# TensorE's instruction order written by the kernel, and the SSD scan as two lanes with GpSimd scaling x and E

## The chip, the cores and the metric

One core of one Trainium2 chip runs the whole program. The metric is the device time of one execution in microseconds (us). The core has TensorE for matrix products (PE in the profile; PEld is its weight load), VectorE (DVE), ScalarE (ACT), GpSimd (POOL), and SyncE (SP), whose queue issues nearly all transfers. PSUM is the accumulator memory that TensorE writes and the other engines read.

## What is computed

The reference is one layer of a diffusion transformer over 1024 latent tokens that follow 256 context tokens, with 2048 channels. Cut to what matters:

```
u = rms_norm(h, pre_w) * (1 + scale) + shift                  # scale, shift, gate from c @ w_ada
z, xbc, dt, qkv, b, a = split(u @ w_in)                       # latent and context rows
xbc, qkv = silu(centred_dwconv(xbc)), silu(centred_dwconv(qkv))
ssd_y = ssd_scan both directions: 16 heads of 64, 2 groups, state 128, chunks of 128
gdn_o = gdn_scan both directions: 8 heads of 128, chunks of 128, per chunk
        (I + strict lower part)^-1 and then, chunk after chunk,
        v_new = u - w @ S;  o = q @ S + attn @ v_new;  S = S * decay + k^T @ v_new
y = concat(ssd_out_norm(ssd_y, z), gdn_out_norm(gdn_o, z))
out = h_lat + gate * rms_norm(y @ w_out, post_w)
```

Both scans run forward and backward over 10 chunks (2 of context, 8 latent), and the context chunks only give the first state.

## The kernel before

The projection `u @ w_in` is worked out in column blocks of 128: 16 z blocks, 24 GDN blocks (q, k, v of 8 heads) and 12 SSD blocks. A column block has two groups of 512 tokens, and for k, v and most SSD blocks a third of 256. Each group is 48 matmuls into one PSUM bank: 16 row blocks of `w_in`, each as three fp16 products (high and low halves). In the rows they read `ps_d<-u,w` or `ps_e<-u,w` (`group`, `products`, L434 to L445). They are called dense products here. What follows a group is VectorE's and ScalarE's work: the convolution (`conv_block`, L498, L502, L503), the split of the next weight tile (`split`, L408, L411, L413), with six buffers of raw weights, five buffers `cv` of convolved blocks (`CB`), and a few PSUM banks.

The rest of the program is put between those blocks. For each GDN head: `gdn_post` (transposes, norms), `gdn_prep` (decay matrices, L676 to L700), `invert` (a recurrence of many small VectorE steps, L726 and L728, then products L764 to L787), `gdn_chain`, `gdn_end`. `gdn_chain` is the recurrence over chunks, for both directions, `ps_c0` and `ps_c1`. A step of one direction is a round trip between engines, three times over: TensorE multiplies with the state S (L850, L852), VectorE forms `r` (L856); TensorE multiplies the inverse with `r` (L866), VectorE forms `xw` (L871) and ScalarE `r`'s successor (L873); TensorE forms the state's increment from `xw` (L876) and the output from `r` (L888), VectorE the new S (L881).

The SSD scan runs in four quarters of four heads (`ssd_quarter`, L915). A quarter first goes backward over its 10 chunks and then forward. Per chunk: `xtok` transposes x; `state` scales it (`xd`, 4 ScalarE instructions, L941), multiplies (L943), multiplies the old state by its decay on GpSimd (L949) and adds on VectorE (L950); `before` multiplies the state with C (L962) and weighs it (L964). The forward direction also builds the 128x128 decay matrices of 4 heads and both directions, `E` (L984 to L996): a broadcast load per direction, 8 ScalarE instructions that add a bias G (L989), two predicated copies and a product on VectorE (L990, L992, L996), an exponential on ScalarE (L991). Four products use E (L1003), GpSimd and VectorE add their parts to the output (L999, L1006).

```
L938 def state(d, c, H, first):
         xd = t_([P, R, PD], "xd", bufs=3)
         for r in range(R): nc.scalar.activation(out=xd[:, r], in_=xs[:, c, r], func=AF.Copy, scale=...)
L982     E = t_([P, 2, R, P], "E", bufs=2)
         for d in range(2): for r in range(R):
L989         nc.scalar.activation(out=E[:, d, r], in_=E[:, d, r], func=AF.Identity, bias=...)
```

`build` (L1201) writes the program as a list of steps (block, post, prep, invert, chain, end, quarter, norm), one wholly behind the other. A scheduler then decides, from costs that it models, in which order each engine gets its instructions, TensorE included; each engine works its own list strictly in that order and waits where an operand is missing. At the end `y @ w_out` is done in 8 column groups of 256 (L1138), with the weights `u<-in_w_out_dram` read and split as before.

## Time and profile before

| what | value |
|---|---|
| median of 3 runs | 2355.13 us (2354.93 to 2360.46) |
| the profiled execution | 2351.73 us, span 2350.0 us |
| mean granted TensorE clock | 0.978 |
| TensorE busy | 2162.5 us, 92% of the span |
| VectorE busy | 1399.5 us, 60% |
| ScalarE busy | 998.5 us, 42% |
| GpSimd busy | 268.7 us, 11% |

The GDN heads lie between about 411 and 1477 us, the SSD scan between about 1500 and 2056 us, and the last product behind that. A wait is put down to the instruction that released it. A matmul in fp32 has two records, and the ends of matmuls are modelled; their starts are what counts.

### The profile page before, as it was taken

Reading aid. Unit: us, or ns where it says so; the run is one execution under the profiler, and the core shown is the slowest. Engines: PE = TensorE matmul, PEld = TensorE weight load, DVE = VectorE, ACT = ScalarE, POOL = GpSimd, SP = SyncE. Lnnn points to the kernel's source line nnn. Section 1 sums busy time; section 2 is a strip of 40 time slices with the busy share of each in tenths; the row PEclk is TensorE's granted clock in tenths of the full one; section 3 lists DMA queues with packets and bytes.
Section 4 is the critical chain, followed back from the end, with each engine's and each line's share of the span. In section 5 each row is a group of like instructions: output and inputs, shape, how many; then the busy total and the mean of one; then the engine's idle time right before and its main releaser. Section 6 shows DMA issues by size and latency. Waiting matters only on the chain. (4 is left out here: it accounts for less than half of the span.)

```text
span 2350.0 us, 41855 instructions
## 1 busy us (share of the span) xinstructions
PE 2162.5 (92%) x16070; PEld 1379.2 (59%) x16070; DVE 1399.5 (60%) x3499; ACT 998.5 (42%) x2493; POOL 268.7 (11%) x514
## 2 busy tenths in 40 slices
PE   4989999889999898998989999999999999899998
PEld 4334644456665655556555566555555555788887
DVE  5335543869694856858568486566767773511214
ACT  6026422344444352433524444465667584423320
POOL 1000001012111020111201110130303130000000
PEclk9999999999999999999999999999999999999999
DMA  9952347454444344343443444333465355212117
GB/s 323 348 164 55 80 145 217 117 131 106 134 115 120 101 126 116 88 133 93 121 119 85 127 123 115 99 90 108 111 183 149 98 164 195 68 37 73 55 37 269
DMA packets 397236, 301.71 MB, mean 128 GB/s; under 512 B 61339, under 2 KB 358684, under 8 KB 395628
## 3 DMA queue, kind: packets, MB, share of 16 engines
q1 hardware_dynamic: 386668, 293.80, 43.7%
q10 hardware_dynamic: 10368, 5.24, 0.8%
q8 instruction: 126, 2.06, 0.4%
q14 instruction: 74, 0.61, 0.1%
HBM read 241.41 MB, written 57.57 MB: 127 GB/s over the span
## 5 line engine op out<-in xcount | busy, mean ns | idle before, releaser
L437 PE MATMUL ps_d<-u,w 128*128 128x512 f16 (+1 forms) x4560 | 969.6, 357 | 8.3 <-DVE cv L498 4.6
L437 PEld LDWEIGHTS <-w 128*128 128x128 f16 x6048 | 595.3, 100 | 494.3 <-issue 36.4
L1138 PEld LDWEIGHTS <-u 128*128 128x128 f16 x3072 | 298.7, 98 | 50.9 <-DMA u<-in_w_out_dram 13.2
L437 PE MATMUL ps_e<-u,w 128*128 128x512 f16 (+1 forms) x1296 | 314.5, 376 | 0.0
L498 DVE SCALAR_TENSOR_TENSOR cv<-ps_d,taps,cv 128x496 f32<-128x496 f32 (+3 forms) x300 | 194.8, 650 | 80.0 <-ACT cv L492 38.6
L413 DVE SCALAR_TENSOR_TENSOR w<-w,scl 128x512 f16<-128x512 f32 (+1 forms) x204 | 149.9, 777 | 50.8 <-ACT w L411 50.3
L408 ACT ACTIVATE w<-w 128x1024 f16<-128x1024 f32 (+1 forms) x102 | 106.5, 1044 | 167.7 <-DMA w<-in_w_in_dram 101.5
L1138 PE MATMUL ps_d<-wx,u 128*128 128x256 f16 x1536 | 170.2, 273 | 4.6 <-DMA u<-in_w_out_dram 4.6
L1138 PE MATMUL ps_d<-w,u 128*128 128x256 f16 x1296 | 144.8, 273 | 5.7 <-DMA u<-in_w_out_dram 3.8
L1168 DVE SCALAR_TENSOR_TENSOR raw<-ps_d,inv,gp 128x256 f32<-128x256 f32 x59 | 28.4, 483 | 193.2 <-ACT jko L1166 193.2
L411 ACT ACTIVATE w<-w,scl 128x1024 f16<-128x1024 f32 (+1 forms) x102 | 112.3, 1133 | 36.2 <-DVE scl L145 16.5
L1166 ACT ACTIVATE jko<-ps_d,inv 128x256 f32<-128x256 f32 x59 | 27.8, 471 | 182.4 <-PE ps_d L1138 177.4
L989 ACT ACTIVATE E<-E,G 128x128 f32<-128x128 f32 x256 | 80.9, 388 | 35.1 <-DMA E<-gr 29.6
L690 ACT ACTIVATE gb<-gb 128x256 f32<-128x256 f32 x80 | 32.2, 413 | 147.0 <-DVE gb L676 144.0
L502 ACT ACTIVATE t<-cv 128x512 f32<-128x512 f32 (+1 forms) x98 | 55.7, 570 | 90.0 <-DVE cv L498 75.4
L676 DVE SCALAR_TENSOR_TENSOR gb<-gb,G,mneg 128x128 f32<-128x128 f32 x160 | 50.8, 345 | 69.2 <-DMA gb<-gr 67.9
L873 ACT ACTIVATE r<-ps_c,nb 128x128 f32<-128x128 f32 x128 | 45.7, 364 | 107.0 <-DVE xw L871 97.2
L876 PE MATMUL ps_c<-xw,vq 128*128 128x128 f32 x288 | 61.8, 304 | 30.8 <-DVE xw L871 14.2
L726 DVE TENSOR_TENSOR tp<-X 80x30 f32<-80x30 f32 (+14 forms) x240 | 77.6, 323 | 13.9 <-DMA X<-d 13.2
L876 PEld LDWEIGHTS ps_c<-xw,vq 128*128 128x128 f32 x288 | 47.4, 196 | 58.9 <-ACT r L873 33.7
L503 DVE SCALAR_TENSOR_TENSOR cv<-t,cv 128x512 f32<-128x512 f32 (+1 forms) x98 | 60.5, 618 | 31.7 <-ACT t L502 31.3
L728 DVE TENSOR_TENSOR X<-X,tp 80x30 f32<-80x30 f32 (+14 forms) x240 | 78.4, 327 | 0.6
(329 smaller groups left out, 3250.4 us busy)
## 6 DMA issues: line engine op xcount, KB each, us to landing
w<-in_w_in_dram SPq DMA_DIRECT2D x102, 512.0 KB
x<-in_w_ada_dram SPq DMA_DIRECT2D x48, 1024.0 KB
vq<-vq SPq DMA_DIRECT2D x128, 256.0 KB
E<-gr SPq DMA_DIRECT2D x64, 256.0 KB
u<-in_w_out_dram SPq DMA_DIRECT2D x24, 512.0 KB
gb<-gr SPq DMA_DIRECT2D x80, 128.0 KB
x<-in_x_dram SPq DMA_DIRECT2D x8, 1024.0 KB
vq<-gb SPq DMA_DIRECT2D x64, 128.0 KB
```

Of the source, the lines that this page charges most:

```text
L408: nc.scalar.activation(out=w16[h][:, 0], in_=w[h], func=AF.Square, accum_out=ssq[:, h:h + 1])
L411: nc.scalar.activation(out=w16[h][:, 0], in_=w[h], func=AF.Copy, scale=t)
L413: nc.vector.scalar_tensor_tensor(out=w16[h][:, 1, s], in0=w[h][:, s], scalar=t, in1=w16[h][:, 0, s], op0=ALU.mult, op1=ALU.subtract)
L437: self.nc.tensor.matmul(out=ps, lhsT=w16[k // KH][:, a, k % KH], rhs=self.u16[b][k][:, lo:lo + n], start=(k == 0 and i == 0), stop=(k == K ...
L498: nc.vector.scalar_tensor_tensor(out=o3[:, :, lo_o:hi_o], in0=p3[:, :, lo_o + s:hi_o + s], scalar=taps[tap], in1=o3[:, :, lo_o:hi_o], op0= ...
L502: nc.scalar.activation(out=t[:, 0:n], in_=o, func=AF.Tanh)
L503: nc.vector.scalar_tensor_tensor(out=o, in0=t[:, 0:n], scalar=1.0, in1=o, op0=ALU.add, op1=ALU.mult)
L726: nc.vector.tensor_tensor(out=t, in0=X[:, k + 1:, k:k + 1].to_broadcast(sh), in1=X[:, k:k + 1, 0:k].to_broadcast(sh), op=ALU.mult)
L728: nc.vector.tensor_tensor(out=X[:, k + 1:, 0:k], in0=X[:, k + 1:, 0:k], in1=t, op=ALU.add)
L876: nc.tensor.matmul(out=pS, lhsT=vq[:, 1], rhs=xw, start=True, stop=True)
L989: nc.scalar.activation(out=E[:, d, r], in_=E[:, d, r], func=AF.Identity, bias=self.G[:, j, c:c + 1])
L1138: self.nc.tensor.matmul(out=ps, lhsT=self.y16(k, p, s), rhs=w16[k // 4][:, q, k % 4], start=(i == 0 and j == 0), stop=(i == KB - 1 and j = ...
```

## The change

TensorE's order is no longer the scheduler's. `mix` takes one generator that emits the dense products one at a time (`dense`), and six others, the lanes, that emit everything else. It keeps a clock of TensorE's own work in nanoseconds (`mm` adds 2 + columns/2.4, four times the columns in fp32), and a lane that yields a number gets its next turn when that many nanoseconds of TensorE work have been emitted. So between two dependent products of a lane lie 2500 ns of other products (`CHAIN`), 3200 (`BACK`) or 5500 (`FORTH`) for the SSD chunks, 2400 per chunk in `gdn_prep`, 40000 ahead of an inverse, 11000 in the split of a weight tile. A lane that yields a condition waits until it holds. The other engines are still ordered by the scheduler. Two rules stop the dense products: a convolved block isn't begun while 5 `cv` buffers are held (`live`), and SSD block 10 not before the SSD buffers exist.

The SSD quarter becomes two lanes, so that the backward half of quarter Q+1 runs beside the forward half of quarter Q. GpSimd scales x (`xd`, 72 instructions of 128x256 for 288 of ScalarE) and adds the bias to E (64 of 128x512 for 256 of ScalarE). E has three buffers for the first direction and one, `E1`, for the second. The gate rows load their weights one group ahead and are spread between dense products. The z blocks 0 to 3 move in front of the SSD blocks. TensorE, VectorE and SyncE issue as many instructions as before.

```diff
+CHAIN, BACK, FORTH = 2500, 3200, 5500
 CB = 5
...
+    def mm(self, out, lhsT, rhs, **kw):
+        n = rhs.shape[-1] if len(rhs.shape) == 2 else rhs.shape[-1] * rhs.shape[-2]
+        self.clock += 2 + n * (4 if rhs.dtype == F32 else 1) / 2.4
+        self.nc.tensor.matmul(out=out, lhsT=lhsT, rhs=rhs, **kw)
+    def mix(self, dense, lanes):
+        self.lanes = [[lane, 0.0] for lane in lanes]
+        self.dense_until = None
+        alive = True
+        while alive or self.lanes:
+            moved = False
+            for it in list(self.lanes):
+                if it[1]() if callable(it[1]) else it[1] <= self.clock:
+                    moved = True
+                    try:
+                        r = next(it[0])
+                        it[1] = r if callable(r) else self.clock + r
+                    except StopIteration:
+                        self.lanes.remove(it)
+            if alive and (self.dense_until is None or self.dense_until()):
+                moved = True
+                try:
+                    self.dense_until = next(dense)
+                except StopIteration:
+                    alive = False
...
+            if not moved:
+                later = [it[1] for it in self.lanes if not callable(it[1])]
...
+                self.clock = min(later)
...
         for k in range(KB):
-            self.products(ps, w16, k, lo, n)
+            for i, (a, b) in enumerate(((0, 0), (0, 1), (1, 0))):
+                self.mm(out=ps, lhsT=w16[k // KH][:, a, k % KH], rhs=self.u16[b][k][:, lo:lo + n],
+                        start=(k == 0 and i == 0), stop=(k == KB - 1 and i == 2))
+                yield
...
+        if pool is None:
+            yield lambda: self.live < CB
+            self.live += 1
...
+            px = ps[:, 2 * P:3 * P]
+            self.mm(out=px, lhsT=D["T"][:, d, c], rhs=r, start=True, stop=True)
...
+                nc.vector.tensor_scalar(out=xw, in0=px, scalar1=D["pw"][:, d, c:c + 1], scalar2=None, op0=ALU.mult)
...
+            yield CHAIN
+            if not last:
+                pS = ps[:, 3 * P:4 * P]
+                self.mm(out=pS, lhsT=vq[:, 1], rhs=xw, start=True, stop=True)
...
+        def scaled(d, c):
+            xd = t_([P, R, PD], "xd", bufs=2)
+            nc.gpsimd.tensor_tensor(out=xd, in0=xs[:, c], in1=bc(self.dtw[:, hs[d], c], PD), op=ALU.mult)
+            return xd
...
+        def within(c):
+            s = slice(c * P, (c + 1) * P)
+            E, E1 = t_([P, R, P], "E", bufs=3), t_([P, R, P], "E1")
+            for d in range(2):
+                nc.sync.dma_start(out=(E, E1)[d], in_=self.gr[hs[d], s].partition_broadcast(P))
+            for d in range(2):
+                nc.gpsimd.tensor_tensor(out=(E, E1)[d], in0=(E, E1)[d], in1=bc(self.G[:, hs[d], c], P), op=ALU.add)
+            nc.vector.copy_predicated(out=E, mask=self.mask[:, 1].bitcast(I32).unsqueeze(1).to_broadcast([P, R, P]), data=E1)
...
+        steps += z(0, 1, 2, 3) + s_(8, 0, 1) + [("W", 0)] + s_(10, 2, 3, 9, 4, 5, 11, 6, 7) + z(4, 5, 6)
...
+        def forth_lane():
+            for Q in range(4):
+                yield until(("B", Q))
+                yield from forth[Q]
+                done.add(("F", Q))
+                if Q < 2:
+                    self.live -= 2 + (Q == 1)
...
+        with tc.manual_schedule(engines={mybir.EngineType.PE}):
+            self.mix(dense(), [chain_lane(0), chain_lane(1), heads_lane(), forth_lane(), back_lane(), first_weights()])
```

On TensorE, in a chunk step of the GDN recurrence of a middle head, before. `ps_c` is a recurrence's bank, `ps_e` that of dense products; a row L866 and the row L876 with the same bank number are the round trip over `xw`:

```order
L866 MATMUL ps_c_6166<-r_6169,A 128x128
L437 LDWEIGHTS w
L437 MATMUL ps_e<-u,w 128x512
L437 LDWEIGHTS w
L437 MATMUL ps_e<-u,w 128x512
L437 LDWEIGHTS w
L437 MATMUL ps_e<-u,w 128x512
L437 LDWEIGHTS w
L437 MATMUL ps_e<-u,w 128x512
L437 LDWEIGHTS w
L437 MATMUL ps_e<-u,w 128x512
L876 MATMUL ps_c_6166<-xw_6174,vq_6135 128x128
```

Five dense products stand between the two here; over the 144 such pairs it is 4 to 6 in half of them, and 0 to 3 in 45.

The same engine and the same kind of place now; all of these products are issued by `mm`, L107. It is one such round trip, of bank 10503, in two pieces:

```order
L107 MATMUL ps_c_10503<-r_10506,A 128x128
L107 LDWEIGHTS w
L107 MATMUL ps_e<-u,w 128x512
L107 MATMUL ps_m<-cv 128x128 x2
L107 LDWEIGHTS w
L107 MATMUL ps_e<-u,w 128x512
```

```order
L107 LDWEIGHTS w
L107 MATMUL ps_e<-u,w 128x512
L107 MATMUL ps_c_10496<-xw_10558,vq_10465 128x128
L107 MATMUL ps_c_10496<-r_10557,vq_10465 128x128
L107 LDWEIGHTS w
L107 MATMUL ps_e<-u,w 128x512
L107 MATMUL ps_c_10503<-xw_10565,vq_10473 128x128
```

Between the two pieces lie four more dense products, eight in all. Of the 144 pairs 102 have 8 to 11 dense products in between, and other lanes' products beside them.

On TensorE where the forward half of SSD quarter 0 runs beside the backward half of quarter 1, now. `ps_x<-ident,cv` are transposes, `ps_z` products with the state, `ps_h` state increments from `xd`, `ps_y` products with E:

```order
L101 MATMUL ps_x<-ident,cv 128x128 x2
L107 MATMUL ps_z<-cv,H_16333 128x128 x2
L107 MATMUL ps_h<-xd,btok 128x256
L107 MATMUL ps_z<-cv,H_16377 128x128 x2
L107 MATMUL ps_y<-E,xs 64x128 x4
L107 MATMUL ps_h<-xd,btok 128x256
L107 MATMUL ps_x<-cv 128x128
```

Rows of this kind stand 108 products long with no dense product between them: five `cv` buffers (SSD blocks 8, 0, 1, 2, 3) are held until the forward half is done. Before, no stretch of the scan is without them.

On GpSimd in the forward half of SSD quarter 0, before (`H` is the state's decay, `cv<-y` the addition to the output):

```order
L949 TENSOR_TENSOR H_16035<-H_15992,cd 128x256
L999 TENSOR_TENSOR cv<-y_16012,cv 128x128 x2
L949 TENSOR_TENSOR H_16078<-H_16035,cd 128x256
L999 TENSOR_TENSOR cv<-y_16055,cv 128x128 x2
L999 TENSOR_TENSOR cv<-y_16098,cv 128x128 x2
```

And now, beside the backward half of quarter 1:

```order
L1064 TENSOR_TENSOR E<-E,G 128x512
L1064 TENSOR_TENSOR E_16566<-E_16566,G 128x512
L1035 TENSOR_TENSOR H_16333<-H_16333,cd 128x256
L1025 TENSOR_TENSOR xd<-xs,dtw 128x256 x2
L1112 TENSOR_TENSOR cv<-y_16501,cv 128x128 x2
L1035 TENSOR_TENSOR H_16663<-H_16592,cd 128x256
L1035 TENSOR_TENSOR H_16333<-H_16333,cd 128x256
```

A pair of chunks, one forward and one backward, now has two additions of 128x512, two scalings and two decays of 128x256 and two additions of 128x128 on GpSimd.

## Rows read from the trace of the kernel before

**Rows 1.** The page: busy time of each engine, share, instructions.
```profile
PE 2162.5 (92%) x16070; PEld 1379.2 (59%) x16070; DVE 1399.5 (60%) x3499; ACT 998.5 (42%) x2493; POOL 268.7 (11%) x514
```

**Rows 2.** Busy us of each engine by stretch, granted clock, DMA share, GB/s.
```profile
core 0: us, PE busy (x) PEld busy (x) DVE busy (x) ACT busy (x) POOL busy (x), PEclk, DMA share, GB/s
...
134.00:411.00 277.00, 253.93 (x1896) 135.12 (x1894) 136.53 (x268) 107.57 (x184) 11.87 (x22) 0.94 0.41 120
411.00:1477.00 1066.00, 986.82 (x7622) 614.82 (x7623) 758.78 (x2189) 427.07 (x1120) 150.56 (x296) 0.97 0.44 116
...
1500.00:2056.00 556.00, 524.26 (x3183) 316.45 (x3181) 362.96 (x746) 343.66 (x898) 89.71 (x153) 0.99 0.44 127
```

**Rows 3.** TensorE's waits between 411 and 1500 us: total, times, longest.
```profile
PE ps_c L888 <- DVE S L881: 14.4, 7, 3.3
PE ps_c L876 <- DVE xw L871: 14.2, 5, 3.2
PE ps_m L693 <- DVE gb L700: 13.8, 7, 6.7
PE ps_c L876 <- ACT r L873: 13.4, 8, 3.0
PE ps_s L134 <- ACT w L408: 9.9, 10, 2.0
PE ps_m L787 <- DVE et L777: 5.2, 8, 0.8
PE ps_c L96 <- POOL o L835: 3.4, 2, 2.0
```

**Rows 4.** TensorE between 763 and 770 us: start, us, instruction, count.
```profile
764.10 1.89 PE L437 MATMUL ps_d<-u,w 128*128 128x512 f16 x8
...
768.74 0.41 PE L850 MATMUL ps_c<-S,cv 128*128 128x128 f32 x2
```

**Rows 5.** VectorE in the same stretch.
```profile
768.51 0.35 DVE L856 SCALAR_TENSOR_TENSOR r<-ps_c,eG,vq 128x128 f32<-128x128 f32 x1
768.82 0.61 DVE L697 SCALAR_TENSOR_TENSOR A<-gb,nb,ps_m 128x128 f32<-128x128 f32 x2
769.40 0.35 DVE L856 SCALAR_TENSOR_TENSOR r<-ps_c,eG,vq 128x128 f32<-128x128 f32 x1
```

**Rows 6.** TensorE's waits between 1500 and 2056 us.
```profile
PE ps_z L962 <- DVE H L950: 6.5, 11, 2.3
PE ps_y L1003 <- DVE E L996: 5.6, 7, 2.2
PE ps_d L437 <- DVE cv L498: 4.6, 3, 2.2
PE ps_h L1047 <- DVE dg L1046: 4.4, 4, 1.5
```

**Rows 7.** Busy us in three slices of 58.75 us, columns as in rows 2.
```profile
528.75:587.50 58.75, 57.80 (x352) 36.87 (x352) 54.24 (x168) 26.97 (x66) 13.72 (x26) 1.00 0.40 106
881.25:940.00 58.75, 50.62 (x546) 35.07 (x545) 39.66 (x117) 16.23 (x34) 0.96 (x2) 0.94 0.48 116
1175.00:1233.75 58.75, 47.30 (x456) 33.23 (x455) 39.86 (x118) 15.13 (x33) 0.95 (x2) 0.95 0.47 119
```

**Rows 8.** GpSimd's groups by shape: busy us, mean ns, idle before.
```profile
L949 POOL TENSOR_TENSOR H<-H,cd 128x256 f32<-128x256 f32 x64 | 47.1, 736 | 114.9 <-ACT H L947 68.0 <-DVE H L950 46.7
L999 POOL TENSOR_TENSOR cv<-y,cv 128x128 f32<-128x128 f32 x64 | 32.2, 524 | 37.3 <-DVE y L964 33.9 <-DMA y<-er 3.5
...
L664 POOL TENSOR_TENSOR cv<-cv,kn 128x512 f32<-128x512 f32 x16 | 19.1, 1194 | 0.6
```

**Rows 9.** SyncE's queue at one chunk of E: start, us, issues.
```profile
1582.02 1.08 SPq L984 DMA_DIRECT2D E<-gr  x2
```

**Rows 10.** ScalarE at the same chunk: start, us.
```profile
1585.86 1.28 ACT L989 ACTIVATE E<-E,G 128x128 f32<-128x128 f32 x4 [2.49 <-DMA E<-gr]
```

**Rows 11.** VectorE's groups between 1500 and 2056 us, columns as in rows 8.
```profile
L950 DVE TENSOR_TENSOR H<-ps_h,H 128x256 f32<-128x256 f32 x64 | 26.7, 417 | 8.8 <-PE ps_h L943 7.3
...
L974 DVE SCALAR_TENSOR_TENSOR cv<-cv,kept,y 128x128 f32<-128x128 f32 x64 | 26.1, 448 | 0.3
L990 DVE COPY_PREDICATED E<-mneg,E 128x512 f32<-128x512 int32 x32 | 24.3, 759 | 20.8 <-ACT E L989 20.8
L992 DVE COPY_PREDICATED E<-ident,dts 128x512 f32<-128x512 int32 x32 | 23.8, 745 | 6.9 <-ACT E L991 6.6
```

**Rows 12.** The page's groups of the weight split on ScalarE.
```profile
L408 ACT ACTIVATE w<-w 128x1024 f16<-128x1024 f32 (+1 forms) x102 | 106.5, 1044 | 167.7 <-DMA w<-in_w_in_dram 101.5
L411 ACT ACTIVATE w<-w,scl 128x1024 f16<-128x1024 f32 (+1 forms) x102 | 112.3, 1133 | 36.2 <-DVE scl L145 16.5
```

**Rows 13.** VectorE from 1500 us: start, us, a weight tile's split.
```profile
1502.46 2.74 DVE L413 SCALAR_TENSOR_TENSOR w<-w,scl 128x512 f16<-128x512 f32 x4 [0.62 <-ACT w L411]
```

**Rows 14.** VectorE between 1554 and 1557 us.
```profile
1554.29 0.34 DVE L974 SCALAR_TENSOR_TENSOR cv<-cv,kept,y 128x128 f32<-128x128 f32 x1
...
1554.89 1.76 DVE L413 SCALAR_TENSOR_TENSOR w<-w,scl 128x512 f16<-128x512 f32 x2
```

**Rows 15.** GpSimd between 1554 and 1557 us.
```profile
1555.05 1.06 POOL L949 TENSOR_TENSOR H<-H,cd 128x256 f32<-128x256 f32 x1 [2.48 <-DVE H L950]
```

**Rows 16.** VectorE between 1557 and 1560 us.
```profile
1557.24 0.96 DVE L974 SCALAR_TENSOR_TENSOR cv<-cv,kept,y 128x128 f32<-128x128 f32 x2
```

**Rows 17.** GpSimd between 1557 and 1560 us.
```profile
1557.40 0.66 POOL L949 TENSOR_TENSOR H<-H,cd 128x256 f32<-128x256 f32 x1 [1.29 <-DVE H L950]
```

580 lines of the change are left out of this document (337 added, 243 removed).

## Prediction

> **What bounds the kernel now.** The page's first part comes first: TensorE is busy 92% of the span, so no other engine is the bound over the whole run [rows 1]. What can be won is TensorE's idle time and the time at a lower clock; the change alters no product. By stretches [rows 2], TensorE idles 277 - 254 = 23 us between 134 and 411, 1066 - 987 = 79 us in the GDN heads, and 556 - 524 = 32 us in the SSD scan. The waits name the causes in the heads: TensorE waits for VectorE's or ScalarE's answer inside the recurrence (14.4, 14.2 and 13.4 us, 20 waits), for the decay matrices (13.8), for the weight split's norm (9.9) and in the inverse (5.2) [rows 3]. The answer itself is quick. A product at 768.74 us [rows 4] has its `r` by 769.40 + 0.35 = 769.75 us [rows 5], 1.0 us later. So TensorE waits where VectorE has something else queued in front. In the SSD scan the waits are many and short, 6.5 us the largest cause [rows 6].
>
> **The GDN heads.** The change puts more cover between dependent products. Eight dense products are issued in 1.89 us, or 0.216 us apart when the modelled last end is left out [rows 4]. Before, 4 to 6 dense products stood between the two products of the `xw` round trip; with other lanes' products that is about 1.5 us. Now 8 to 11 stand there, about 2.8 us (counted, here and below, as 0.216 us for a dense product of 512 columns and 0.22 for one of 128 columns in fp32). So 1.3 us goes from each of the 13 waits for `xw` and `r` (17 of 27.6 us). For the 7 waits on S the cover rises less, from about 2.1 to 2.9 us, so some 0.8 us each, 6 of 14.4. The 42 us become 19; I put 4 back, since an even spacing also shortens the longest covers that the scheduler had given. The decay matrices get 2.4 us per chunk where the longest wait was 6.7 us: half, 7 us, stays. The weight split's norm gets 11 us against waits of at most 2.0, so 1 us stays. The inverse and the remaining small waits go from about 17 to 7. Sum 82 to 38 us, **-44**. Bounds: -15 if VectorE's bursts are as long as before behind a fixed order, -70 if hardly a wait remains. Nothing hides a loss here: behind a TensorE instruction that waits, the whole list waits, dense products too.
>
> At the end of head 7 there is no dense product left to put between (20 products, about 3.5 us, each link about 1.0 us): **+6**. The granted clock is 0.97 in the heads, so 32 us of that window are lost to it [rows 2]. It was 1.00 in a slice where TensorE idled 1 us and 0.94 and 0.95 in slices where it idled 8 and 11 [rows 7]; with half the idle time gone I take a third of the loss back, **-10** (0 to -20). Between 134 and 411 us the gate rows are now spread with their weights loaded a group ahead: of 23 us idle I take **-6** (0 to -15). The heads and what is ahead of them together: **-54**.
>
> **The SSD scan.** Here a cost appears that the trace of before hasn't got. Where forward 0 runs beside backward 1, TensorE has 108 products of at most 0.24 us, about 20 us by their columns, and no dense product: the `cv` buffers hold those back until the lane is done. What ends last is then GpSimd. Per pair of chunks it gets two additions of 128x512, four operations of 128x256 and two of 128x128: 2 x 1.19 + 4 x 0.74 + 2 x 0.52 = 6.4 us [rows 8]. Eight pairs are 51 us; the first E are done earlier, so about 47 us, 27 beyond TensorE's 20. Some conflict with VectorE (below) makes it **+30** (20 to 43). The single buffer E1 is nearly as slow: from issue [rows 9] to use [rows 10] 3.8 us, then 1.19 and a copy of 0.76 [rows 11], 5.8 us per chunk. ScalarE's part is less than before and waits for no one.
>
> Forward 2 beside backward 3 has 8.1 us of TensorE per pair against the 6.4: **+4** (0 to 9). Forward 1 stands nearly alone, 7.0 us against 2 x 1.19 + 2 x 0.74 + 2 x 0.52 = 4.9 us: **+2**. Forward 3 has only the last z products and w_out's first weights beside it, 3.5 to 5 us a chunk against E1's 5.8: **+8** (2 to 17). Behind it, the last pieces of w_out's first weights can be loaded only when the last state is done: a load longer than E's 3.8 us, then square 1.04 and scale 1.13 us [rows 12] and a split, with one chunk beside it: **+9** (5 to 15). The old waits: 3.2 to 5.5 us now lie between a chunk's products, and the 20.8 us that VectorE waited for ScalarE's additions to E [rows 11] are gone as a cause; of 32 us idle I let half go, **-16** (-10 to -24). After the stretch without dense products the clock may be low for a while: **+3**. Sum **+40**. The SyncE queue issues as many loads as before, and no lane waits on it in a new place but for E1.
>
> **The sum.** -54 + 40 = -14 us on the profiled execution's own 2351.7 us gives 2338 us. That execution lies 3.4 us below the median of the runs shown, less than the 0.3% (7 us) that a measurement of this kernel can tell from no change. I keep **2338**.
>
> **A rule weighed.** In the trace, VectorE and GpSimd do get in each other's way. Four weight splits on VectorE took 2.74 us, 0.69 each [rows 13]; two of them with a GpSimd decay in flight took 1.76 us [rows 14], where 1.4 would be expected, and that decay took 1.06 us [rows 15] against 0.66 [rows 17]. The pair of additions in [rows 16] took 0.96 us, with a GpSimd operation in flight, where one alone takes 0.34 [rows 14]. The Trainium skill, page "SBUF — State Buffer", section "SBUF: two separate sides", says that a VectorE operation with two operands in SBUF and a GpSimd operation take one port pair as an exclusive lock, and the second blocks for the whole instruction. The trace agrees in kind, but each lost 0.35 to 0.4 us and not the other's whole length. By the rule taken fully, the time is that of the first rival; by the rows, it is inside the +30. The Trainium skill, page "GPSIMD Engine Reference", section "Engine selection", also advises against GpSimd for elementwise work with two inputs, about 2 times slower; the trace has 736 ns [rows 8] against VectorE's 417 for the same shape [rows 11], 1.8 times. The sum above already goes by the 736 ns.
>
> **The rivals.**
> *GpSimd and VectorE exclude each other, slower.* Per pair VectorE has two operations on E of 128x512 and two additions of 128x128, 0.76 + 0.75 + 2 x 0.34 = 2.2 us. If they add wholly to GpSimd's, a pair takes 8.6 us with the means of rows 8, or 8.0 with 0.66 for the undisturbed decays. Then the stretch without dense products costs 8 x 8.0 - 20 = 44; forward 2, with a share of the weight split on top, 9.2 - 8.1 over 8 chunks, 9; forward 1 costs 8, forward 3 17, the end 14. With -16 and +3 that is +79, and -54 + 79 = +25: **2377**. For it: rows 14 to 17. Against it: not the whole length is lost there. It decides from the point where the scan gives back more than the 54 us of the heads. That is visible in VectorE's 128x512 copies at 1.2 us or more.
> *VectorE's list sets the pace, slower.* Its order is still the scheduler's, by modelled costs, against a TensorE order that no longer gives way. In a slice VectorE was busy 54 of 58.75 us [rows 7]. If its bursts (four splits, 2.74 us [rows 13]) come ahead of an answer, the 2.8 us don't suffice and the waits only move: -15 in place of -44, clock -5: -20 + 40 = +20, **2372**. Against it: in that slice TensorE idled 1 us.
> *More is won.* The waits fall to 15 us (-67), the clock gives 18, head 7 costs 3, the gate rows -8, sum -90; the stretch costs 22, forward 3 4, the end 5, old waits -20, other 3, sum +14. Total -76: **2276**. For it: a free answer takes 1.0 us, so 2.8 us is ample.
> *The order isn't what it says.* TensorE's list as built shows it, so this has 2 in 100, with no change, 2352.
>
> **How the numbers follow.** Forecast 0.40 (2315 to 2362), exclusion 0.24 (2360 to 2400), VectorE's list 0.11 (2360 to 2385), more won 0.23 (2260 to 2305), no change 0.02. A tenth left out at each end: about half of what more won holds lies below 2280, and somewhat over a quarter of the two slow cases above 2386. Range 2280 to 2386. Faster by over 0.3% is below 2348: 0.72 of the forecast and all of more won, 0.52. Within: 0.19 of the forecast, a bit of the slow cases and the no change, 0.14. Slower 0.34.
>
> **What would show it.** Right: TensorE's waits for S, `xw` and `r` fall from 42 to about 23 us and the norm's wait is gone; clock 0.98 in the heads; a stretch of 45 to 55 us in the scan with TensorE busy 20, GpSimd over 80% busy and 6 to 7 us between its pairs. Wrong: that stretch near 25 us, or 65; waits of the recurrence still over 40 us; a wait of over 20 us ahead of w_out.

## The result, and the profile after

The changed kernel takes 2526.1 us (2519.2 to 2529.6, 4 runs) against 2357.8 us (2354.9 to 2362.9, 4 runs): 1.071 times as long, interval 1.0675 to 1.074. That is 168 us slower, where 14 us faster was forecast, and 140 us outside the range. The profiled execution took 2529.6 us, span 2527.8, granted clock 0.941 (before 0.978).

The page of the kernel after gives each engine's busy time, as [rows 1]:

```profile
PE 2199.7 (87%) x16070; PEld 1424.3 (56%) x16070; DVE 1417.6 (56%) x3499; ACT 860.3 (34%) x1949; POOL 380.8 (15%) x650
```

The number of TensorE instructions is the same, and none of the engines is busier in share but GpSimd. The span is 178 us longer, and 141 us of that are idle time of TensorE: 2527.8 - 2199.7 = 328 us, where it was 187.5. The other 37 us are the same products taking longer. From 134 us on, both kernels are cut at the same places of the program: at the first and at the last product of the inverse with `r`, and at the first product of `w_out`. The rows are the stages ahead of the recurrence, of the GDN heads and of the SSD scan, first of the kernel before, then after, columns as in [rows 2]:

```profile
134.00:499.10 365.10, 333.38 (x2529) 175.09 (x2528) 204.41 (x452) 145.60 (x266) 15.48 (x30) 0.94 0.42 117
499.10:1478.00 978.90, 908.36 (x6998) 575.55 (x6997) 691.54 (x2009) 389.59 (x1040) 147.62 (x292) 0.98 0.44 116
1478.00:1983.10 505.10, 478.61 (x2718) 271.70 (x2718) 335.31 (x692) 315.36 (x838) 90.41 (x158) 0.99 0.46 130
```

```profile
134.00:507.50 373.50, 335.25 (x2540) 180.54 (x2533) 207.00 (x448) 144.85 (x250) 15.27 (x29) 0.93 0.40 111
507.50:1601.60 1094.10, 958.55 (x7235) 613.31 (x7235) 719.60 (x2050) 407.65 (x1077) 148.77 (x293) 0.95 0.39 106
1601.60:2156.40 554.80, 458.57 (x2478) 269.11 (x2478) 320.54 (x654) 159.78 (x273) 201.58 (x293) 0.91 0.40 117
```

Products moved between the stages (237 records more in the heads, 240 fewer in the scan), so the stages' lengths can't be compared directly. So for each stage the issue time is added up that its products take when nothing holds them, and the rest is called lost. The issue time is 0.216 us for 512 columns in fp16, as in [rows 4], and in proportion for fewer; a record in fp32 counts twice its columns; small tiles, of which several run side by side, count the median spacing that they have in the kernel before. In the heads 978.9 - 845.1 = 134 us are lost before and 1094.1 - 884.3 = 210 after; in the scan 505.1 - 445.4 = 60 and 554.8 - 404.1 = 151. So the heads lose 76 us more and the scan 91; ahead of the heads it is 6 more, in the last product 5, together the 178 us of the span. The issue times are estimates from the spacing, good to a few us. Part of the loss is the clock: what the products that began at the lower clock took beyond their issue time, waits left out, went from 22 to 43 us in the heads and from 5 to 35 in the scan.

TensorE's waits in the heads of the kernel after (total, times, longest), beside [rows 3]:

```profile
PE ps_c L107 <- ACT r L951: 40.0, 26, 7.3
PE ps_c L107 <- DVE o L969: 34.6, 17, 7.4
PE ps_c L107 <- DVE o L937: 19.2, 10, 7.8
PE ps_m L836 <- DMA xc<-d: 15.8, 3, 8.1
PE ps_c L107 <- ACT o L940: 12.2, 8, 2.7
```

The four `ps_c` rows are the recurrence: 106 us, against 42 before. There were waits of up to 3.3 us; now there are some of 7 to 8. The norm of the weight split, 9.9 us before, is gone, as forecast. The decay matrices have fallen to one wait of 3.2 us, ahead of the heads' first product. The inverse's waits have grown: the 15.8 us for its load (`xc<-d`) are three waits. So the longer cover was given where the program says, and the recurrence nevertheless waits longer. Two places of the kernel after show why.

**A load that stands behind a store.** TensorE waits three times here for the recurrence (start, us, instruction, count, idle before and its releaser):

```profile
816.26 0.49 PE L107 MATMUL ps_c<-r,A 128*128 128x128 f32 x2 [2.38 <-ACT o L940]
...
822.58 0.80 PE L107 MATMUL ps_c<-xw,vq 128*128 128x128 f32 x2 [3.23 <-ACT r L951]
...
827.44 0.80 PE L107 MATMUL ps_c<-xw,vq 128*128 128x128 f32 x2 [3.63 <-ACT r L951]
```

VectorE in the same stretch, and then SyncE's queue:

```profile
814.55 0.35 DVE L746 SCALAR_TENSOR_TENSOR gb<-gb,G,mneg 128x128 f32<-128x128 f32 x1 [4.10 <-DMA gb<-gr]
...
815.41 0.60 DVE L932 SCALAR_TENSOR_TENSOR r<-ps_c,eG,vq 128x128 f32<-128x128 f32 x2
...
820.28 0.61 DVE L746 SCALAR_TENSOR_TENSOR gb<-gb,G,mneg 128x128 f32<-128x128 f32 x2 [4.27 <-DMA gb<-gr]
...
821.79 0.34 DVE L949 TENSOR_SCALAR xw<-ps_c,pw 128x128 f32<-128x128 f32 x1
...
826.37 0.35 DVE L746 SCALAR_TENSOR_TENSOR gb<-gb,G,mneg 128x128 f32<-128x128 f32 x1 [4.24 <-DMA gb<-gr]
```

```profile
802.63 0.81 SPq L772 DMA_DIRECT2D vq<-gb  x1
...
810.12 0.36 SPq L756 DMA_DIRECT2D gb<-gr  x1
```

The chain of waits (start, us, what) has at that place:

```profile
802.63 7.48 DMA vq<-gb
```

Read from the bottom: the load into a `gb` buffer (L756) may be issued only when the store out of the same buffer (L772) has landed, and the one of 802.63 took 7.48 us; the load goes out at 810.12. It takes about 4 us, and VectorE stands nearly all that time (4.10 us) at the instruction that reads it, L746. Behind it on VectorE's list lie the recurrence's `r` and `xw`, whose operands were there before: `r` is formed at 815.41, at once after the stop. Then comes the next stop. Such stops on VectorE (total, times, longest), before and after:

```profile
DVE gb L676 <- DMA gb<-gr: 67.9, 31, 4.2
```

```profile
DVE gb L746 <- DMA gb<-gr: 84.7, 38, 4.3
```

So they were there before, and 33 of the 48 us that TensorE then waited in `ps_c` overlap a stop or the 3 us behind it. After, it is 54 of 109 us.

**A burst of VectorE's own work.** TensorE in the kernel after:

```profile
1329.55 0.39 PE L107 MATMUL ps_c<-r,vq 128*128 128x128 f32 x2
...
1339.45 0.79 PE L107 MATMUL ps_c<-S,cv 128*128 128x128 f32 x2 [7.36 <-DVE o L969]
```

VectorE meanwhile, without a stop; four of its 25 rows between 1329.0 and 1339.2 us:

```profile
1330.88 0.74 DVE L479 SCALAR_TENSOR_TENSOR w<-w,scl 128x512 f16<-128x512 f32 x1
...
1335.76 0.73 DVE L569 SCALAR_TENSOR_TENSOR cv<-ps_d,taps,cv 128x504 f32<-128x504 f32 x1
...
1337.66 0.34 DVE L964 SCALAR_TENSOR_TENSOR S<-S,cd,ps_c 128x128 f32<-128x128 f32 x1
...
1339.12 0.28 DVE L969 TENSOR_TENSOR o<-ps_c,o 128x128 f32<-128x128 f32 x1
```

TensorE waits for the new S and for L969, which reads the bank last; both operands were there when the product of 1329.55 was done. Ahead of them VectorE's list has a weight tile's split (four L479), four convolution steps (L569) and nine steps of the inverse (L797, L799), 8 us in all. S itself takes 0.34 us. Summed over all waits in `ps_c`, 109 us after: in 25 of them VectorE worked on splits, in 19 on convolutions, in 13 on inverse steps, in 17 on the decay matrices (L746, L768, L771); in 11 it stood at a `gb`, in 4 it was idle for another cause, and 20 are the chain's own work.

In the scan, two windows of the kernel after: forward 0 where it has no dense products, and forward 3 with what follows it:

```profile
1715.00:1772.00 57.00, 39.16 (x190) 29.45 (x191) 40.02 (x88) 9.57 (x18) 39.99 (x59) 0.71 0.40 110
...
2063.00:2150.00 87.00, 55.41 (x287) 30.36 (x287) 48.71 (x91) 20.00 (x30) 31.13 (x43) 0.82 0.49 153
```

The first is the stretch that the prediction gave 47 us; it is 57 us long, GpSimd busy 40 of them, the granted clock 0.71. TensorE's waits of the whole scan (after):

```profile
PE ps_z L107 <- DVE H L1036: 22.5, 12, 4.9
PE ps_s L1158 <- DVE E L1155: 14.2, 1, 14.2
PE ps_z L107 <- DVE y L1053: 12.1, 7, 3.3
PE ps_s L183 <- ACT jkw L1238: 9.5, 1, 9.5
```

The second is new, a single wait in forward 3. It is the sum of squares for the scan's output norm, whose operands come through SyncE's queue. Two pieces of the chain of waits there:

```profile
2080.78 3.77 DMA y<-p
...
2091.42 4.16 DMA xs<-yr
```

The stores of the half worked on before land one after another, then the next half is loaded, and only then come its products and squares; TensorE's list stands at the sum from 2088 to 2102. The sum's tile shares the one buffer E1, so the next E1 is loaded only behind it, and forward 3 stands still too. The fourth wait is the scale of `w_out`'s first weights, at 2144 to 2154 us.

### The profile page after: what moved, and what is told of

The parts are those of the page before. It is cut to its first block, busy times and chain, and to the rows that moved or that the text cites. A ratio compares the mean times of both kernels' runs of the same rounds, so it can differ in the third digit from the quotient of the medians.

```text
span 2527.8 us, 41463 instructions
## 1 busy us (share of the span) xinstructions
PE 2199.7 (87%) x16070; PEld 1424.3 (56%) x16070; DVE 1417.6 (56%) x3499; ACT 860.3 (34%) x1949; POOL 380.8 (15%) x650
## 4 chain that ended last, share of the span: by engine, by line
PE 52%; DVE 19%; DMA 17%; issue 5%; POOL 4%; ACT 3%; SPq 1%; ACTq 0%; POOLq 0%; DVEq 0%
PE ps_d L107 19%; PE ps_d L1263 11%; PE ps_e L107 6%; DMA vq<-gb 4%; PE ps_c L107 3%; DMA gb<-gr 3%; DMA E<-gr 3%; DVE cv L569 3%; DVE w L479 2%; DVE X L799 2%; DVE tp L797 2%; PE ps_m L380 2%; POOL E L1064 1%; DMA u<-in_w_out_dram 1%; PE ps_d L300 1%
## 5 line engine op out<-in xcount | busy, mean ns | idle before, releaser
L107 PE MATMUL ps_d<-u,w 128*128 128x512 f16 (+1 forms) x4464 | 958.3, 363 | 6.0 <-DVE cv L569 3.1
L107 PEld LDWEIGHTS <-w 128*128 128x128 f16 x5760 | 573.1, 101 | 490.5 <-issue 55.6
L107 PE MATMUL ps_e<-u,w 128*128 128x512 f16 (+1 forms) x1296 | 306.2, 377 | 0.0
L569 DVE SCALAR_TENSOR_TENSOR cv<-ps_d,taps,cv 128x496 f32<-128x496 f32 (+3 forms) x304 | 200.4, 659 | 66.9 <-ACT cv L563 37.8
L479 DVE SCALAR_TENSOR_TENSOR w<-w,scl 128x512 f16<-128x512 f32 (+1 forms) x204 | 145.0, 762 | 19.6 <-ACT w L477 19.5
L746 DVE SCALAR_TENSOR_TENSOR gb<-gb,G,mneg 128x128 f32<-128x128 f32 x160 | 52.3, 348 | 84.7 <-DMA gb<-gr 84.7
L107 PE MATMUL ps_c<-xw,vq 128*128 128x128 f32 x288 | 58.8, 295 | 41.6 <-ACT r L951 40.0
L107 PE MATMUL ps_c<-S,cv 128*128 128x128 f32 x288 | 58.2, 289 | 35.9 <-DVE o L969 34.6
L1064 POOL TENSOR_TENSOR E<-E,G 128x512 f32<-128x512 f32 x64 | 71.8, 1125 | 98.1 <-DMA E<-gr 69.8
L107 PE MATMUL ps_c<-r,A 128*128 128x128 f32 x288 | 58.0, 289 | 31.8 <-DVE o L937 19.2
L797 DVE TENSOR_TENSOR tp<-X 80x30 f32<-80x30 f32 (+14 forms) x240 | 79.1, 330 | 10.7 <-DMA X<-d 7.3
L799 DVE TENSOR_TENSOR X<-X,tp 80x30 f32<-80x30 f32 (+14 forms) x240 | 80.1, 334 | 3.7
L107 PEld LDWEIGHTS ps_c<-xw,vq 128*128 128x128 f32 x288 | 47.8, 197 | 59.1 <-ACT r L951 51.9
```

The source lines that it names most:

```text
L107: self.nc.tensor.matmul(out=out, lhsT=lhsT, rhs=rhs, **kw)
L479: nc.vector.scalar_tensor_tensor(out=w16[h][:, 1, s], in0=w[h][:, s], scalar=t, in1=w16[h][:, 0, s], op0=ALU.mult, op1=ALU.subtract)
L569: nc.vector.scalar_tensor_tensor(out=o3[:, :, lo_o:hi_o], in0=p3[:, :, lo_o + s:hi_o + s], scalar=taps[tap], in1=o3[:, :, lo_o:hi_o], op0= ...
L746: nc.vector.scalar_tensor_tensor(out=e, in0=e, scalar=self.G[:, 32 + d * 8 + h, c:c + 1], in1=self.mneg[:, d], op0=ALU.subtract, op1=ALU.min)
L797: nc.vector.tensor_tensor(out=t, in0=X[:, k + 1:, k:k + 1].to_broadcast(sh), in1=X[:, k:k + 1, 0:k].to_broadcast(sh), op=ALU.mult)
L799: nc.vector.tensor_tensor(out=X[:, k + 1:, 0:k], in0=X[:, k + 1:, 0:k], in1=t, op=ALU.add)
```

## The experiments

The theory: TensorE's fixed order is what costs, because VectorE's and SyncE's lists are still the scheduler's and TensorE no longer gives way when one of their answers is late. The first rival: GpSimd for x and E, which lengthens the scan and delays VectorE. The second: the numbers of nanoseconds between the steps are too small, or too large. Each run is given against the kernel before on the same chip, since this varied from 2346.5 to 2359.2 us among the chips. A single run of the kernel before differs from its median by up to 11 us, so single runs that differ by less than about 12 us tell nothing.

| run | us | before | difference |
|---|---|---|---|
| the changed kernel | 2526.1 | 2357.8 | +168 |
| e1, order of TensorE by the scheduler | 2401.1 | 2347.8 | +53 |
| e4, x and E on ScalarE | 2507.2 | 2347.8 | +159 |
| e9, e1 and e4 | 2361.9 | 2346.5 | +15 |
| e17, e9 and product of `gb` in own buffers (6 runs) | 2325.4 | 2350.5 | -25 |
| e18, e17 with the fixed order | 2464.9 | 2350.5 | +114 |

**e1: TensorE's order left to the scheduler.** The lanes still set the order in which the program is written.

```diff
-        with tc.manual_schedule(engines={mybir.EngineType.PE}):
+        with ExitStack():
```

> The changed kernel, only the block that fixes TensorE's order is taken away: the same program, lanes and GpSimd work, but the scheduler orders TensorE again as it did before. Theory A (the fixed order is what costs, since it doesn't give way where VectorE or a load is late): the loss of 170 us mostly goes, 2350 to 2420 us, recurrence waits back under 60 us. Theory B (the other parts cost: lanes, GpSimd, one E1, the rule on the cv buffers): 2480 us or more.

Measured: 115 of the 168 us go. The heads lose 130 us, about as much as in the kernel before (134). TensorE's waits in the heads:

```profile
PE ps_c L107 <- ACT r L951: 24.1, 15, 4.5
PE ps_c L107 <- DVE o L969: 14.3, 8, 3.4
```

All waits in `ps_c` are 53 us now, where they were 109. VectorE's stops at `gb` are hardly shorter (77 us), but TensorE has dense products in front of the waiting product. The scan still loses 118 us (151 with the fixed order, 60 before): there it isn't the order alone.

**e2, e3, e7, e14: the spacing and the buffers.** e2: `GB` 4 to 8, twice the `gb` buffers. e3: 5000 for 2400 in `gdn_prep`. e7: `CHAIN` 3500 for 2500. e14: `CHAIN` 1800.

```diff
-GB = 4
+GB = 8
```

```diff
-            yield 2400
+            yield 5000
```

```diff
-CHAIN, BACK, FORTH = 2500, 3200, 5500
+CHAIN, BACK, FORTH = 3500, 3200, 5500
```

> The changed kernel with 8 buffers gb in the heads in place of 4, nothing else. Theory A1 (in the heads a load of gb waits for the store of the buffer four chunks before; VectorE waits for that load, 84.7 us in all, with the recurrence's steps behind it in its list): VectorE's waits for gb fall under 30 us, TensorE's waits in the recurrence from 106 us by 50 or more, time 2435 to 2470. Theory A2 (the 2.5 us between dependent products are too little against VectorE's bursts of weight split and convolution): within 15 us of 2526.

> The changed kernel with 5000 in place of 2400 ns of TensorE work between the chunks of the decay matrices. Theory A1: a load and a store of gb now have time to land, VectorE's waits for gb fall to under 40 us and the time by 40 to 80 us, less what a head's inverse that starts 26 us later costs. Theory A2: no change or slower, 2515 to 2550.

> The changed kernel with CHAIN 3500 in place of 2500. If the answers are late by a few us beyond 2.8 in some sixty places, each place gains up to 1 us: 2470 to 2505. If they are late by so much that 1 us is little, or later chains push the heads back: 2515 to 2550.

> The changed kernel with CHAIN 1800 in place of 2500. If the distance of 2.5 us hides the answers and 3500 lost only because the longer recurrence ran into the next head's work: then 1800 loses cover, 2530 to 2570. If the length of the recurrence is what costs at any distance (it overlaps with the next head's decay matrices and their stops): 2470 to 2515.

Measured: +152, +247, +270 and +150 us against before; so -17, +79, +102 and -18 against the changed kernel. The ranges expected of e2, e3 and e7 were all missed; e14 came out as its second. More time between dependent steps makes it worse: with `CHAIN` 1800, 2500 and 3500 the waits in `ps_c` are 76, 109 and 148 us. The rows are, in order, a wait of e3 (TensorE) and one of e7 (VectorE):

```profile
PE ps_m L836 <- DMA xc<-d: 80.9, 7, 14.4
```

```profile
DVE gb L746 <- DMA gb<-gr: 116.3, 43, 6.7
```

In e3 the inverse begins later and its load is waited for in the open; in e7 the recurrence of a head lasts longer, lies beside the next head's decay matrices and their stops (84.7 to 116.3 us), and twice there is no dense product for 26 and 28 us (10.6 at most in the changed kernel). Another 38 us of its waits are for a `ps_c` bank that the end of the previous head empties late (L990). The heads take 1183 us instead of 1094. Eight buffers help little: SyncE still waits 113 us for stores of `gb` (143 in the changed kernel), and VectorE's stops fall only to 63 us. The loads stand close behind stores there too, presumably because the scheduler places them earlier.

**e5: the product of `gb` in buffers of its own.** So the load needn't wait until the store has landed.

```diff
-                nc.vector.tensor_tensor(out=gb, in0=gb, in1=pk[:, P:2 * P]....to_broadcast([P, 2, P]), op=ALU.mult)
-                nc.sync.dma_start(out=D["vq"][:, c, 0:5:4], in_=gb)
+                gs = t_([P, 2, P], "gs", bufs=4)
+                nc.vector.tensor_tensor(out=gs, in0=gb, in1=pk[:, P:2 * P]....to_broadcast([P, 2, P]), op=ALU.mult)
+                nc.sync.dma_start(out=D["vq"][:, c, 0:5:4], in_=gs)
```

> The changed kernel, where the product of gb with q and k goes to 4 buffers gs of its own and is stored from there, so that a load of gb waits for VectorE's reading alone and not for a store to land. In the changed kernel 54 of the 110 us that TensorE waits in the recurrence come up to 3 us behind a stop of VectorE for a load of gb, 56 do not. Theory A1 (loads behind stores): VectorE's stops for gb fall from 85 to under 30 us, time 2465 to 2495. Against it (the stop only moves to the next thing that is late): 2510 or more.

Measured: +124 us against before, 44 less than the changed kernel. VectorE's stops:

```profile
DVE gb L746 <- DMA gb<-gr: 54.7, 30, 4.2
```

The loss in the heads falls from 210 to 165 us. Of the idle time in `ps_c`, 19 us lie at or behind a `gb` stop (54 without the edit) and 62 elsewhere (56). So these stops were worth 44 us, and 81 of the 109 us of waits stay. The stops themselves fell less than expected (under 30).

**e13: half of the split from VectorE to ScalarE, on e5.** The edit leaves out the subtraction: the second half of a split weight holds the high part again and not the rest. The number and the shapes of the products stay, so only the time is of use.

```diff
-                nc.vector.scalar_tensor_tensor(out=w16[h][:, 1, s], in0=w[h][:, s], scalar=t, in1=w16[h][:, 0, s],
-                                               op0=ALU.mult, op1=ALU.subtract)
+                nc.scalar.activation(out=w16[h][:, 1, s], in_=w[h][:, s], func=AF.Copy, scale=t)
```

> The run with buffers gs (2475 us), where ScalarE writes the low half of each split weight in VectorE's place. It writes the high half again and not the rest, so the products come out less exact; their number and shapes stay. VectorE loses 200 instructions of 0.74 us, ScalarE gets them at about 0.6. If bursts of VectorE work ahead of an answer make the waits that are left: 30 to 60 us less, 2415 to 2445. If they do not: 2465 to 2485.

Measured: 2457.1 us, +98 against before, 26 less than e5, between the two expectations. The waits in `ps_c` fall from 81 to 69 us. So with the splits off VectorE a part of the waits goes, and the bursts of convolution and inverse stay. It isn't a clean test: ScalarE has more to do, and VectorE's stops at `gb` are 74 us again.

**e6: VectorE's order written too.** If the scheduler's VectorE list doesn't fit TensorE's, both may be taken from the program.

```diff
-        with tc.manual_schedule(engines={mybir.EngineType.PE}):
+        with tc.manual_schedule(engines={mybir.EngineType.PE, mybir.EngineType.DVE}):
```

> The changed kernel with VectorE's order written by the kernel too: each VectorE instruction stands where the lanes emit it, an answer right behind the product it answers. Theory A2 (VectorE's list is the scheduler's, and puts 8 to 10 us of weight split, convolution and inverse ahead of an answer that TensorE's fixed list needs): the 56 us of recurrence waits without a load fall under 20, the SSD waits too, 2430 to 2475. Against it (bursts of VectorE work are there in any order, and a strict list makes VectorE itself wait for dense groups): 2520 to 2600.

Measured: 2949.5 us, +599 against before. TensorE's wait and VectorE's in the heads:

```profile
PE ps_c L107 <- ACT r L951: 170.7, 24, 32.9
```

```profile
DVE tp L797 <- DMA X<-d: 68.9, 7, 15.6
```

In written order, VectorE stands up to 15.6 us at the load with which an inverse begins, while the recurrence's answers lie behind it, and TensorE stands behind those. The written order names no time for a transfer; a list that stops at loads needs one. Neither expectation came. The seven stops are 69 us; what the rest of the 599 is made of was not separated.

**e4, e8, e11: GpSimd for x and E.** e4 takes the two edits out of the changed kernel, e8 puts them into the kernel before, e11 only the one for x. In e8:

```diff
-            for r in range(R):
-                nc.scalar.activation(out=xd[:, r], in_=xs[:, c, r], func=AF.Copy, scale=...)
+            nc.gpsimd.tensor_tensor(out=xd, in0=xs[:, c], in1=bc(self.dtw[:, hs[d], c], PD), op=ALU.mult)
...
-                    for r in range(R):
-                        nc.scalar.activation(out=E[:, d, r], in_=E[:, d, r], func=AF.Identity, bias=...)
+                    nc.gpsimd.tensor_tensor(out=E[:, d], in0=E[:, d], in1=bc(self.G[:, hs[d], c], P), op=ALU.add)
```

> The changed kernel with x and E scaled by ScalarE again (288 and 256 instructions), two lanes and the fixed order kept. If GpSimd's load sets the SSD scan: the stretch without dense products falls from 57 to some 40 us, forward 3 from 80 to 65, in all 25 to 40 us less, 2485 to 2500. If the waits of the lanes themselves set it (round trips without cover, one E1, loads): within 10 us, 2515 to 2535.

> The kernel before with only GpSimd in ScalarE's place for x and E (72 and 64 instructions for 288 and 256). If exclusion of GpSimd and VectorE or GpSimd's slowness is what the SSD scan loses by: 10 to 30 us slower than before. If it is the lanes without dense products: within 6 us of before.

> The kernel before with only x scaled by GpSimd (72 instructions of 0.67 us, 48 us of the 120 that moved in the run with both). If GpSimd's time or its exclusion with VectorE costs, about 20 us in proportion, 2368 to 2375. If the cost is GpSimd's list standing at a load of E (66 us in that run) with the decays and x behind it: within 6 us of before.

Measured: e8 +58 us, e11 +17, so about 41 for E, from single runs. In the changed kernel the two edits cost 168 - 159 = 9 us, which these single runs don't tell from nothing, though the scan loses 134 us in e4 and not 151; with the scheduler's order they cost 53 - 15 = 38. All of e8's loss lies in the scan (111 us lost against 60; the heads' 979.6 us are the same). Waits in the scan of e8, of VectorE and GpSimd:

```profile
DVE E L987 <- POOL E L986: 48.8, 25, 4.8
```

```profile
POOL E L986 <- DMA E<-gr: 66.4, 30, 8.6
```

GpSimd's list now stops at the loads of E, 30 times, and has decays and scaled x behind them. VectorE, which stood 20.8 us for ScalarE's additions [rows 11], stands 48.8 for GpSimd's. The operations also grow. A group of VectorE's and the window of the whole scan in e8:

```profile
L987 DVE COPY_PREDICATED E<-mneg,E 128x512 f32<-128x512 int32 x32 | 28.5, 891 | 48.8 <-POOL E L986 48.8
```

```profile
1480.80:2039.00 558.20, 496.38 (x2733) 279.87 (x2733) 349.03 (x694) 174.59 (x297) 210.78 (x294) 0.96 0.41 119
```

The copy, L990 in the kernel before, was 759 ns [rows 11] and is 891. But VectorE's whole work in the scan grew from 335.3 us (692 instructions) to 349.0 (694), so the lengthening on VectorE comes to 14 us at most, and not all of it is waited for; the stops at loads and for GpSimd are several times larger. They aren't the whole, though: in e11 no load of E stands in GpSimd's list, and it came out near its first expectation, GpSimd's time or its exclusion with VectorE. How much of the 58 us each of these brings was not separated: three buffers for E in the kernel before, which would have brought its loads forward, were not tried.

**e12: a z block put into the stretch without dense products.**

```diff
-        steps += z(0, 1, 2, 3) + s_(8, 0, 1) + [("W", 0)] + s_(10, 2, 3, 9, 4, 5, 11, 6, 7) + z(4, 5, 6)
+        steps += z(0, 1, 2) + s_(8, 0, 1) + [("W", 0)] + s_(10, 2, 3) + z(3) + s_(9, 4, 5, 11, 6, 7) + z(4, 5, 6)
```

> The changed kernel with z block 3 placed behind SSD block 3 instead of ahead of block 8: it needs no cv buffer, so its 96 dense products stand in the stretch of forward 0 that had none (26 us of products without a dense one become 7; at the end of head 7 it becomes 11 from 4). If missing dense products are the stretch's loss: forward 0 falls from 57 us by 15 or more beyond its added 21 us of products, total 2500 to 2515. If GpSimd's pace is: 2520 to 2530.

Measured: +173 us against before on its chip, 2519.4 us in all, no difference that a single run can tell. Forward 0 then takes 60 us with 21 us more of dense products in it, so the stretch was filled, and the scan loses 133 us where it lost 151. But the heads and the stage ahead of them lose 9 us more, so hardly any of it reaches the total.

**e10, e15: own buffers in the kernel before.** The edit of e5 in the kernel before.

> The kernel before with the product of gb stored from 4 buffers gs of its own. Before, 33 of the 47 us that TensorE waits in the recurrence come up to 3 us behind a stop of VectorE for gb. If loads behind stores make those stops: 10 to 30 us faster, 2320 to 2340. If the scheduler's order has already moved TensorE's products away from them: within 5 us of before.

> The kernel before with the buffers gs again, timed. One look gave 2338 against 2347 us. If loads behind stores cost the kernel before too: ratio 0.995 to 0.998, its interval below 1. If that look was chance: interval around 1.

Measured: e10 -8 us, one run; e15 2345.1 us (7 runs) against 2359.2 (12), ratio 0.994, interval 0.992 to 0.996. The same stops exist there and cost 14 us, clear of noise though under 1%; behind the fixed order they cost 44.

**e9, e16, e17, e18: the parts put together.** e9 is e1 with e4. e16 and e17 are one kernel, e9 with e5's edit. e18 is the same with the fixed order, on e17's chip.

> The changed kernel with the scheduler's order on TensorE again and x and E on ScalarE again; lanes, buffers and the order of blocks stay changed. With the scheduler's order alone it took 2401 us, and GpSimd alone cost the kernel before 58 us. If the two parts are the whole loss: 2340 to 2358 us. If ScalarE gives back only the 19 us that it gave under the fixed order, and the lanes hold the rest: 2378 to 2395.

> Lanes, block order and buffers of the change, with the scheduler's order, ScalarE and the buffers gs. Without gs it took 2362 us. If gs helps as it helped the kernel before: 2350 to 2356. If the lanes make the heads wait for loads more than before: 2335 to 2348.

> The same kernel as e16, timed: lanes, block order and buffers of the change, the scheduler's order on TensorE, x and E on ScalarE, buffers gs. By the look of e16 against before on its chip: ratio 0.986 to 0.992. If that look was a lucky run: 0.994 to 1.0, no better than gs in the kernel before.

> As e17, but TensorE's order written by the kernel as in the change. If order, GpSimd and loads were three separate losses: the order's own, some 85 us or more, remains, 2420 to 2460. If the order only costs because of the loads and GpSimd: 2335 to 2370.

Measured: e9 +15 us; e16 2332.6 against 2359.2; e17 2325.4 (2322.8 to 2328.4) against 2350.5 (2340.8 to 2356.3), ratio 0.990, interval 0.9875 to 0.992; e18 2464.9. So the fixed order costs 140 us where everything else is as in e17 (159 - 15 = 144 without the own buffers, 115 with GpSimd too). It is thus a loss of its own, as the first expectation of e18 had it, whose range ends 5 us below. Waits of the recurrence in the heads of e17 are down to a few, 29 us in all:

```profile
PE ps_c L107 <- DVE o L970: 9.5, 10, 3.0
PE ps_c L107 <- ACT o L941: 8.7, 6, 2.7
```

The heads and the scan, first of e17, then of e18, columns as in [rows 2]:

```profile
490.30:1465.40 975.10, 927.36 (x7250) 598.62 (x7250) 711.19 (x2050) 408.39 (x1076) 153.28 (x294) 0.99 0.43 119
1465.40:1961.00 495.60, 441.60 (x2521) 260.33 (x2521) 313.05 (x658) 311.02 (x839) 86.05 (x156) 0.96 0.46 135
```

```profile
507.60:1562.50 1054.90, 946.52 (x7234) 611.43 (x7234) 716.15 (x2050) 407.75 (x1076) 149.24 (x293) 0.96 0.40 110
1562.50:2097.00 534.50, 451.90 (x2479) 265.00 (x2480) 305.75 (x655) 305.12 (x817) 87.28 (x157) 0.92 0.41 121
```

VectorE does the same work in both (711 and 716 us in the heads). With its list scheduled together with TensorE's, TensorE idles 48 us there; with TensorE's list written apart, 108, and the recurrence waits 81 us, during which VectorE was at convolutions 19, splits 18 and inverse steps 12 us, idle only 3. This is the second place above, nearly without the stops at `gb`. The lanes, the order of the blocks and the spread gate rows, without the fixed order and without GpSimd but with the own buffers, beat both kernels. Of these 25 us the buffers alone give 14 in the kernel before (e15). The scan of e17 still loses 88 us, where the kernel before loses 60, so what is left of the change costs time in the scan.

What isn't shown is whether some other written order would do as well: only this one, with its spacing varied, was tried.

## Why the prediction was wrong

**The step that failed is the heads' -44.** It set the cover, 2.8 us of products, against an answer of 1.0 us and let each wait shrink by the added cover. That holds if the answer comes at a fixed time after the product. Here it comes when VectorE's list reaches it: 4 us late at the first place above, 8 at the second. The recurrence waits 106 us and not 23, and with the clock the heads and the stage ahead of them lose 82 us more in place of 54 less. The rival that said so, *VectorE's list sets the pace*, got 0.11 and 2372. It was right in its mechanism: e1, e17 and e18 show it, and the parts taken out in e5 and e13 agree. But its bound of -15 still took the waits to fall. What it lacked: the scheduler's order put TensorE's dense products ahead of late answers, and the fixed order gives that up (115 to 144 us); none of the three spacings tried gave it back. The evidence held against it, a slice of [rows 7] where VectorE is busy 54 of 58.75 us and TensorE idles 1, fits that effect and is no sign that bursts do no harm.

**A second omission: stops at loads.** The part on SyncE counted the loads and said that no lane waits on it in a new place. The place is old, 67.9 us of VectorE's stops before, and most of the 42 us that the prediction set out to shorten lay at or behind one: what kept VectorE there was a load. What is new is how long TensorE stands behind VectorE. e5 gives it 44 us. The rows on VectorE's waits for transfers were not among those that the prediction used.

**What came as forecast.** The norm's wait is gone, the decay matrices took 3.2 us instead of the 7 allowed. Against an even share of what the scan lost before, forward 2 lost some 5 us more (4 forecast), what follows the last state 12 (9). The stretch without dense products took 57 us, longer than the 45 to 55 named. It lost 36 us, some 33 more than its share, against the +30. That is close in part by luck, since it wasn't GpSimd alone: GpSimd was busy 40 of 57 us, 70% and not over 80. About 14 of the 36 us are products at half clock, where the prediction had +3 for the whole scan.

**Terms that were mis-sized.** The clock: -10 in the heads against +21 measured, +3 in the scan against +30; the low clock stands where TensorE idles, so in the heads this follows from the failed step. The inverse's and the small waits were to fall to 7 us and are 26. The stage ahead of the heads lost 6 us more in place of 6 less. Forward 3 lost some 30 us more and not 8, with the 14.2 us wait at the norm's sum in it. Between the last chunk step and forward 0 some 16 us more are lost, and the sum has no term for it. The 16 us of old waits were not obtained: TensorE waits 22.5 us for H at `ps_z` alone, and in e8, where only GpSimd's work is changed, 25.8 where it was 6.5 [rows 6]. The first rival's 2377 was for GpSimd against VectorE. In the kernel before, the two edits do cost 58 us, but its mechanism, the length of the operations, holds 14 us of VectorE's at most.

The rule behind that rival holds here all the same, and the prediction misread its rows. The Trainium skill, page "SBUF — State Buffer", section "SBUF: two separate sides", says that of a GpSimd operation and a VectorE operation with two inputs in SBUF the one that starts first keeps a shared pair of ports for its whole instruction and the other is blocked. The trace of e8 agrees. Of the 32 copies on E at L987, 14 take 0.73 to 0.75 us. The other 18 begin while a GpSimd operation on two tiles is under way, and last longer by what is left of it, less 0.15 us: 0.19 to 0.20 more with 0.34 us left, 0.23 to 0.25 with 0.38, 0.40 with 0.55. GpSimd is held up in its turn. One such place in e8, GpSimd and then VectorE:

```profile
1700.74 0.62 POOL L948 TENSOR_TENSOR H<-H,cd 128x256 f32<-128x256 f32 x1
1701.32 1.50 POOL L986 TENSOR_TENSOR E<-E,G 128x512 f32<-128x512 f32 x1
```

```profile
1700.81 1.13 DVE L987 COPY_PREDICATED E<-mneg,E 128x512 f32<-128x512 int32 x1 [2.86 <-POOL E L986]
```

The copy waits out the decay and takes 1.13 us for 0.73; the addition behind it waits out the copy and takes 1.50 for 1.05. So the 0.35 to 0.4 us in rows 14 to 17 were the rest of an operation that was already under way: the second split of [rows 14] began with 0.56 us of the decay to go. What the rule costs is small because of that, 14 us of VectorE's work in e8's scan. The sign that the prediction gave, copies of 1.2 us or more, came once in 32 in the changed kernel (1.57 us).

## What to carry to other kernels

Cover between two dependent products is worth something only against the place of the answer in the answering engine's list: look at what that engine does during the wait, before counting products. Be wary of fixing one engine's order while the others are scheduled; here it cost 115 to 144 us, and fixing a second engine's order without times for its loads cost 430 more. A buffer that is loaded, worked on in place and stored from holds its next load behind the store's landing, so give the result a buffer of its own where the loading engine's list has anything urgent behind it.

## What was not expected of the hardware

A store of two 128x128 tiles took 7.48 us to land (802.63 us, after); the load behind it was there 4.4 us after its issue. Idle time is paid a second time: in the stretch from 1715 us TensorE was idle 18 of 57 us and its granted clock was 0.71, so part of its work ran at the lower of its two levels, 1.2 GHz; in the scan as a whole the clock went from 0.99 to 0.91. GpSimd was not slowed by its larger share: its decays of 128x256 had a mean of 736 ns [rows 8], and 710 in e8's scan. Most of them took 0.62 to 0.67 us in both; the means are raised by 22 of 64 before and 11 in e8, which took 0.9 to 1.2 us.
